# A hybrid decoder layer on one core: two row pairs of each output-projection half by Strassen's scheme

## The chip, the cores and the metric

The kernel runs on one core of a Trainium2 chip. The metric is the device time of one execution in microseconds (us); of several runs the median is given. TensorE (PE) multiplies, VectorE (DVE) and ScalarE (ACT) do the elementwise work, GpSimd (POOL) and SyncE (SP) here issue transfers. Each engine works through its own instructions in order.

## The reference

One layer on 256 rows of width 2048, all in float32. The change sits in the line `h = h + concat(A, B) @ w_o`, the output projection.

```python
a = rmsnorm(h, attn_norm[i])
proj = a @ w_in[i]                       # q, latent, rope key, q, k, v of two head groups
out_mla  = mla_attention(...)            # group A: 8 heads of 128
out_moba = moba_attention(...)           # group B: 8 heads of 128
h = h + jnp.concatenate([out_mla, out_moba], axis=-1) @ w_o[i]     # 2048 x 2048
f = rmsnorm(h, ffn_norm[i])
h = h + (jax.nn.silu(f @ w_gate[i]) * (f @ w_up[i])) @ w_down[i]   # inner width 5632
g = jax.nn.sigmoid(rmsnorm(h, ple_norm[i]) @ w_ple_gate[i])
h = h + g * (p[i] @ w_ple_proj[i])
return rmsnorm(h, final_norm)
```

## The kernel before

**Three matmuls for one.** Every float32 operand is split into a high part (rounded to the matmul's type fp32r) and a low part (what the rounding left). A product is three matmuls: high by high, low by high, high by low (lines 388, 389, 390). So each weight that comes from memory passes through ACT (the cast at line 337 writes the high part) and then DVE (the subtraction at line 348 writes the low part) before PE may use it.

**Units.** A matrix product is a `group`: 1024 columns of the weights, two row tiles of 128 tokens, and a list of units. A unit is a pair of 128-row blocks of the weights: 1 MB, loaded by SP into one of three buffers `raw` (tiles 112, 113 and 114 in the program; two more from the feed-forward part on). Its parts lie in a ring of 12 places of 512 columns (`ringh`, `ringl`); a group marked `deep` has four more places (`moreh`, `morel`). A plain unit takes four places and 24 matmuls of 512 columns.

**Strassen's scheme.** A unit is two blocks of weights by two halves of columns, against two by two blocks of activations, so Strassen's seven products can take the place of eight: 21 matmuls instead of 24. This asks for sums of the weights (lines 347, 350, 351, on DVE, in the buffer itself) which have to be split as well: seven places of the ring instead of four. It also asks for four sums of the activations (lines 140 to 143 in `act_transpose`, or `sums_of`), and at the end of a run of such units four additions that gather the products from PSUM into a tile `U` (lines 466 to 469). `seven` runs such a unit in four turns; its four extra PSUM banks are all that the other work has, so while a run lasts nothing else may take a bank. Before the change the feed-forward groups and the last projection use it; the output projection, `wo0` and `wo1` (columns 0 to 1023 and 1024 to 2047), consists of 16 plain units.

**Early sums.** For 13 of the feed-forward Strassen units the sums of the weights are made ahead: `early_sums` loads the weights by POOL's queue, adds on DVE (lines 372 to 374) and stores the sums to memory, from where they are loaded later. The last two of them (units 5 and 6 of `u4`, used near the end of the feed-forward part) are made while the output projection runs.

**Order around the change.** The output projection begins while the second attention group is still in its softmax. The values of the heads are multiplied between the first four units of `wo0` (lines 620, 621), and their parts `oB` are written by ACT and DVE (lines 106, 107). Tasks that wait for a turn (`add`, `step`) are woven between the units. When `wo0` is done, its four banks are added to the residual `h` (line 918), ACT sums the squares, and `ffn_norm_half(0)` takes the root of the norm, scales `h` (line 971), turns it on PE (line 123) and makes the parts and the sums of the next activations, one pair for each of the last units of `wo1`. When `wo1` is done the same happens for the second half, during the first units of the gate projection `g0`.

Of the kernel before, what the change touches and what calls it, by code (L numbers as in the profile page):

```python
# [8 lines left out]
F32 = mybir.dt.float32  # L9
# [4 lines left out]
ALU = mybir.AluOpType  # L14
# [21 lines left out]
def kernel(ctx, tc, x, w_in, w_ukv, w_o, w_gate, w_up, w_down, w_ple_gate, w_ple_proj,  # L36
                             final_norm, x_turned, p_turned, columns_in, out):
    nc = tc.nc
# [73 lines left out]
    def act_transpose(src, k0, g0, dst, kd0=None, scaled=False, sums=None):  # L112

        kd0 = k0 if kd0 is None else kd0
        part = src[:, :, k0 * 128:k0 * 128 + 256]
        if scaled:
            part = S["nrm"][:, (k0 // 2) % 2]
        b = obank()  # L120
        for i in range(2):
            for t in range(NT):
                nc.tensor.transpose(b[:, (2 * i + t) * 128:(2 * i + t + 1) * 128],  # L123
                                    part[:, t, i * 128:(i + 1) * 128], ident)
# [12 lines left out]
        a11, a21, a12, a22 = (whole[:, i, t * 128:(t + 1) * 128] for i in range(2) for t in range(2))
        four = some.rearrange("q a (b c) -> q (a b) c", b=2)
        tt = nc.vector.tensor_tensor
        tt(four[:, 0], a21, a22, op=ALU.add)  # L140
        tt(four[:, 2], a21, a11, op=ALU.subtract)
        tt(four[:, 1], four[:, 0], a11, op=ALU.subtract)
        tt(four[:, 3], a12, four[:, 1], op=ALU.subtract)
        split_psum(sums[0], sums[1], four)

    def square_sum(src, acc):
# [22 lines left out]
    units = []  # L169
# [169 lines left out]
    def split_lo(jb, c0=0, c1=None, n=1, row=slice(None)):  # L339

        if units[jb.unit].adding:
            return
        h, l, r = (x[:, row] for x in by_row_tile(n, *parts_of(jb), raw_of(jb)))
        tt = nc.vector.tensor_tensor
        f = quarters(jb) if jb.kind == "21" and not units[jb.unit].early else None
        if f is not None:
            tt(f[:, 0:2], f[:, 1:2].to_broadcast([128, 2, 512]), f[:, 0:4:3], op=ALU.subtract)  # L347
        tt(l[:, :, c0:c1], r[:, :, c0:c1], h[:, :, c0:c1].bitcast(F32), op=ALU.subtract)  # L348
        if f is not None:
            tt(f[:, 3], f[:, 3], f[:, 0], op=ALU.subtract)  # L350
            tt(f[:, 2], f[:, 2], f[:, 3], op=ALU.subtract)  # L351

    todo_early = []

    def early_sums(tag, enough, wait, landed=None):

        made = 0
        while todo_early and made < enough:
            u = todo_early.pop(0)
            made += 1  # L360
            f = big.tile([128, 4, 512], F32, name="wsums", tag=tag)
            (w, c0, _), k0 = u.srcs[0], u.ks[0] * 128
            if landed is not None:
                nc.gpsimd.tensor_copy(f[:, 0, 0:1], landed)
                landed = None
            nc.gpsimd.dma_start(f.rearrange("q (k a) c -> q k (a c)", k=2),
                                w[k0:k0 + 256, c0:c0 + 1024].rearrange("(k q) c -> q k c", q=128))
            since = columns[0]
            while columns[0] < since + wait() or S["crowded"]:
                yield 1  # L370
            tt = nc.vector.tensor_tensor
            tt(f[:, 0:2], f[:, 1:2].to_broadcast([128, 2, 512]), f[:, 0:4:3], op=ALU.subtract)
            tt(f[:, 3], f[:, 3], f[:, 0], op=ALU.subtract)
            tt(f[:, 2], f[:, 2], f[:, 3], op=ALU.subtract)
            u.early = dram.tile([128, 2048], F32, name=f"wsums{u.name}{u.idx}")
            nc.gpsimd.dma_start(u.early, f.rearrange("q a c -> q (a c)"))
# [65 lines left out]
    def seven(u, turn):  # L442
        st = u.st
        if turn == 0 and u.sevens_first:
            take_banks(u)
            n = B["next"] % 4
            st["free"] = B["rot"][n:] + B["rot"][:n]
            B["rot"], B["next"] = [st["banks"][1, 1]] if u.first else [], 0
            st.update(zip(("m1", "m7", "m5", "m6"), st["free"]))
        h, l = u.turns[turn][0].h, u.turns[turn][0].l  # L450
        k = u.ks[0]
        a11, a12, a22 = u.lhs(k, 0), u.lhs(k + 1, 0), u.lhs(k + 1, 1)
        s1, s2, s3, s4 = (u.sums(k, j) for j in range(4))
        todo = (((0, "m1", a11), (1, "m3", s4)), ((0, "m2", a12),), ((1, "m7", s3), (0, "m5", s1)),
                ((1, "m6", s2), (0, "m4", a22)))[turn]
        alone = {"m2": (0, 0), "m3": (1, 0), "m4": (0, 1)}
        for q, m, xs in todo:
            b = st["banks"][alone[m]] if m in alone else st[m]
            three(b, xs, h[:, 512 * q:512 * q + 512], l[:, 512 * q:512 * q + 512], begins(u, alone.get(m, m)),
                  u.sevens_end and m not in alone)  # L460
        if turn == 3 and u.sevens_end:
            U = S["U"] = big.tile([128, NT, 1024], F32, name="U", tag="vb")
            c1, c2 = U[:, :, 0:512], U[:, :, 512:1024]
            tt = nc.vector.tensor_tensor
            nc.scalar.copy(c1[:, 0], st["m1"])
            tt(c2[:, 0], c1[:, 0], st["m6"], op=ALU.add)
            tt(c1[:, 1], c2[:, 0], st["m7"], op=ALU.add)
            tt(c2[:, 0], c2[:, 0], st["m5"], op=ALU.add)
            tt(c2[:, 1], c1[:, 1], st["m5"], op=ALU.add)
            B["rot"], B["next"] = st["free"], 0  # L470
            if u.into is not None:
                def join(hs=S["h"][:, :, u.into:u.into + 1024]):
                    tt(hs, hs, U, op=ALU.add)
                    yield 1
                add(join())

    def sums_of(parts, k0, pairs, at, tag="vb"):

        for n, kk in enumerate(pairs):
            both = big.tile([128, 2, 2, SEQ], F32, name="both", tag=tag)  # L480
            whole, some = both[:, 0], both[:, 1]
            h, l = (x[:, kk - k0:kk - k0 + 2] for x in parts)
            tt = nc.vector.tensor_tensor
            tt(whole, h.bitcast(F32), l.bitcast(F32), op=ALU.add)
            a11, a21, a12, a22 = (whole[:, i, t * 128:(t + 1) * 128] for i in range(2) for t in range(2))
            hi, lo = (aT[i][:, at + 2 * n:at + 2 * n + 2] for i in range(2))
            four = some.rearrange("q a (b c) -> q (a b) c", b=2)
            tt(four[:, 0], a21, a22, op=ALU.add)
            tt(four[:, 1], four[:, 0], a11, op=ALU.subtract)
            tt(four[:, 2], a21, a11, op=ALU.subtract)  # L490
            tt(four[:, 3], a12, four[:, 1], op=ALU.subtract)
            split_psum(hi, lo, some)
            yield 1

# [9 lines left out]
    def add(gen, wait=0, front=False):  # L504
        tasks.insert(0 if front else len(tasks), [wait, gen])
# [450 lines left out]
    def ffn_norm_half(k0):  # L956

        def after():
            def g():
# [38 lines left out]
    def a_sums(k, j):  # L998
        return tuple(S["sums"][i][k // 2][:, j] for i in range(2))

    group("wo0", [(wo, 0, 1024)], K16, C2, o_l, add_evac(0, ssh, ffn_norm_half(0)))
    group("wo1", [(wo, 1024, 2048)], K16, C2, o_l, add_evac(1024, ssh, ffn_norm_half(8)), swap=True, deep=True)


    ffT = {}
# [323 lines left out]
    for i, u in enumerate(units):  # L1329
# [5 lines left out]
        S["long"] = u.name in ("ga", "q0", "u0", "wo0", "wo1")  # L1335
        S["crowded"] = u.name == "v" and u.idx > 0 or u.name == "wo0" and u.idx < 4
        if u.name == "ga" and u.idx == 5:
            todo_early.extend(x for x in units if x.early)
            add(early_sums("f0l", 2, lambda: 53248, raw[i + 3][:, 0, 0:1]))
        if u.name == "ga" and u.idx == 8:  # L1340
            add(early_sums("more_sums", 99, lambda: 57344 if S["long"] else 34816))
        if u.name == "g1" and u.idx == 0:
            S["mid"] = S.pop("turned")
        if u.name == "wo0":
# [87 lines left out]
```

## Time and profile before

| | |
|---|---|
| median of 3 runs | 1181.11 us (1179.98 to 1181.36) |
| the profiled execution | 1180.28 us, of which the span from first to last instruction is 1178.5 us |
| output projection on PE | first matmul at 285.27 us; `wo1` begins at 334.95 us |
| PE, DVE, ACT busy over the span | 99%, 81%, 60% |
| data moved | 287.80 MB, mean 244 GB/s |
| granted TensorE clock | 0.998 |

Times in the trace are microseconds from the start of the span. A row of the timeline gives start, duration, engine, line, operation, output and input tile, the shape, and how many equal instructions it merges; in brackets, how long the engine had stood idle and who ended that. A row of windows gives a stretch, its length, and the busy time of PE, PE's weight loads, DVE, ACT and POOL.

### The profile page before, as it was taken

The numbers are of one execution on the slowest core, as the hardware profiler recorded it, in microseconds if no ns is written. First come the engines' busy times: TensorE is split into PE (matmuls) and PEld (weight loads), VectorE is DVE, ScalarE is ACT, GpSimd is POOL, SyncE is SP. The second block draws the span as 40 slices with busy tenths as digits, with TensorE's granted clock in tenths as the row PEclk, the third lists the DMA queues.
The fourth block names the chain that finished last, engine by engine and source line by source line (L and its number), as shares of the span: only waits on it lengthen the run. The fifth ranks groups of instructions, "written<-read, shape, count | busy, mean of one in ns | idle before, by whom it ended". The sixth has DMA issues, their size and how long they took to land.

```text
span 1178.5 us, 14590 instructions
## 1 busy us (share of the span) xinstructions
PE 1167.4 (99%) x5477; PEld 978.3 (83%) x5477; DVE 952.9 (81%) x1127; ACT 710.7 (60%) x898; POOL 50.2 (4%) x73
## 2 busy tenths in 40 slices
PE   9999999999999999999999999999999999999996
PEld 7888888899888888888888888888888888888886
DVE  6866756776557689999999899989998989897474
ACT  6745746456456756667566666757575756465453
POOL 5000000000000000000000000000000000000000
PEclk9999999999999999999999999999999999999999
DMA  9896787755683776686959596868868795846531
GB/s 328 298 337 202 288 299 258 267 185 206 220 330 130 280 260 220 235 283 208 353 171 334 154 348 210 291 214 321 240 214 255 283 276 195 326 153 218 201 107 72
DMA packets 85880, 287.80 MB, mean 244 GB/s; under 512 B 5681, under 2 KB 7985, under 8 KB 81201
## 3 DMA queue, kind: packets, MB, share of 16 engines
q1 hardware_dynamic: 76352, 239.71, 56.7%
q0 software_dynamic: 8880, 46.14, 14.2%
q10 hardware_dynamic: 576, 1.02, 0.3%
q8 instruction: 43, 0.70, 0.2%
q14 instruction: 29, 0.23, 0.1%
HBM read 252.24 MB, written 26.21 MB: 236 GB/s over the span
## 4 chain that ended last, share of the span: by engine, by line
PE 95%; DMA 2%; ACT 1%; DVE 1%; SPq 0%; issue 0%; ACTq 0%; DVEq 0%
PE bank L390 30%; PE bank L388 30%; PE bank L389 30%; DMA raw<-in_w_in 2%; PE bank L591 1%; PE bank L1052 1%; PE bank L123 1%; PE bank L620 1%; ACT ringh L337 1%; PE bank L614 0%; PE bank L594 0%; PE bank L726 0%; DMA xT<-in_x_turned 0%; PE bank L621 0%; ACT aT L109 0%
## 5 line engine op out<-in xcount | busy, mean ns | idle before, releaser
L337 ACT CAST ringh<-raw 128x1024 fp32r<-128x1024 f32 (+5 forms) x310 | 372.7, 1239 | 274.9 <-PE bank L389 112.0
L348 DVE TENSOR_TENSOR ringl<-raw,ringh 128x1024 fp32r<-128x1024 f32 (+5 forms) x310 | 444.7, 1457 | 101.9 <-ACT ringh L337 100.0
L388 PE MATMUL bank<-ringh,aT 128*128 128x512 f32 (+3 forms) x713 | 274.7, 385 | 0.2
L390 PE MATMUL bank<-ringl,aT 128*128 128x512 f32 (+3 forms) x713 | 270.8, 380 | 0.0
L389 PE MATMUL bank<-ringh,aT 128*128 128x512 f32 (+3 forms) x713 | 270.3, 379 | 0.0
L390 PEld LDWEIGHTS bank<-ringl,aT 128*128 128x128 f32 x713 | 134.1, 188 | 25.3 <-DVE ringl L348 0.9
L388 PEld LDWEIGHTS bank<-ringh,aT 128*128 128x128 f32 x713 | 134.2, 188 | 24.7 <-ACT ringh L337 1.0
L389 PEld LDWEIGHTS bank<-ringh,aT 128*128 128x128 f32 x713 | 134.3, 188 | 23.8 <-DVE aT L658 0.2
L337 ACT CAST moreh<-raw 128x1024 fp32r<-128x1024 f32 (+2 forms) x70 | 79.8, 1173 | 19.9 <-DVE raw L347 9.2
L348 DVE TENSOR_TENSOR morel<-raw,moreh 128x1024 fp32r<-128x1024 f32 (+2 forms) x66 | 85.5, 1317 | 1.8 <-ACT moreh L337 1.3
L388 PE MATMUL bank<-ringh,ffTh 128*128 128x512 f32 x204 | 79.5, 390 | 0.0
L337 ACT CAST most<-raw 128x1024 fp32r<-128x1024 f32 (+2 forms) x58 | 56.8, 1005 | 37.5 <-DVE raw L347 14.4
L390 PE MATMUL bank<-ringl,ffTh 128*128 128x512 f32 x204 | 79.4, 389 | 0.0
L389 PE MATMUL bank<-ringh,ffTl 128*128 128x512 f32 x204 | 79.4, 389 | 0.0
L348 DVE TENSOR_TENSOR most<-raw,most 128x1024 fp32r<-128x1024 f32 (+2 forms) x58 | 66.3, 1164 | 1.6 <-ACT most L337 1.5
L347 DVE TENSOR_TENSOR raw<-raw 128x1024 f32<-128x1024 f32 x51 | 62.5, 1225 | 1.7
L389 PEld LDWEIGHTS bank<-ringh,ffTl 128*128 128x128 f32 x204 | 38.3, 188 | 8.0
L388 PEld LDWEIGHTS bank<-ringh,ffTh 128*128 128x128 f32 x204 | 38.3, 188 | 7.9
L390 PEld LDWEIGHTS bank<-ringl,ffTh 128*128 128x128 f32 x204 | 38.3, 188 | 7.9
L351 DVE TENSOR_TENSOR raw<-raw 128x512 f32<-128x512 f32 x51 | 35.3, 692 | 1.8
L350 DVE TENSOR_TENSOR raw<-raw 128x512 f32<-128x512 f32 x51 | 34.9, 684 | 0.0
L388 PE MATMUL bank<-most,aT 128*128 128x512 f32 x88 | 34.6, 394 | 0.0
(356 smaller groups left out, 1958.6 us busy)
## 6 DMA issues: line engine op xcount, KB each, us to landing
raw<-in_w_down SPq DMA_DIRECT2D x44, 1024.0 KB, 7.2
raw<-in_w_gate SPq DMA_DIRECT2D x35, 1024.0 KB, 7.4
raw<-in_w_up SPq DMA_DIRECT2D x32, 1024.0 KB, 7.5
raw<-in_w_in SPq DMA_DIRECT2D x40, 512.0 KB, 5.4
raw<-in_w_o SPq DMA_DIRECT2D x16, 1024.0 KB, 5.6
raw<-in_w_ple_gate SPq DMA_DIRECT2D x16, 1024.0 KB, 5.0
raw<-in_w_in SPq DMA_DIRECT2D x8, 1024.0 KB, 5.0
wsums<-in_w_up POOLq DMA_DIRECT2D x8, 1024.0 KB, 7.1
```

Of the source, the lines that this page charges most:

```text
L123: nc.tensor.transpose(b[:, (2 * i + t) * 128:(2 * i + t + 1) * 128], part[:, t, i * 128:(i + 1) * 128], ident)
L337: nc.scalar.copy(h[:, :, c0:c1], r[:, :, c0:c1])
L347: tt(f[:, 0:2], f[:, 1:2].to_broadcast([128, 2, 512]), f[:, 0:4:3], op=ALU.subtract)
L348: tt(l[:, :, c0:c1], r[:, :, c0:c1], h[:, :, c0:c1].bitcast(F32), op=ALU.subtract)
L350: tt(f[:, 3], f[:, 3], f[:, 0], op=ALU.subtract)
L351: tt(f[:, 2], f[:, 2], f[:, 3], op=ALU.subtract)
L388: nc.tensor.matmul(b, xh, h, start=start, stop=False)
L389: nc.tensor.matmul(b, xl, h, start=False, stop=False)
L390: nc.tensor.matmul(b, xh, l, start=False, stop=stop)
L591: nc.tensor.matmul(s[:, c0:c0 + nk], qT[:, q * 128:(q + 1) * 128], kT[:, 0:nk], start=True, stop=qpe is None)
L620: nc.tensor.matmul(o[:, 0:256], v(0), pT[:, 0:256], start=True, stop=False)
L1052: nc.tensor.transpose(b[:, (2 * i + t) * 128:(2 * i + t + 1) * 128], st[:, t, (k + i) * 128:(k + i + 1) * 128], ident)
```

## The change

Two units of `wo0` (heads 4 and 5, and 6 and 7, of the first attention group) and the same two of `wo1` become Strassen units, at places 4 and 5 of `wo0` and 2 and 3 of `wo1`. Their activations' sums are made by `sums_of` when `wo0` reaches its fourth and fifth unit, into a part of `aT` that is free then, and serve both halves. After each run the gathered tile `U` is added to `h` by one instruction (`join`). `ffn_norm_half(0)` takes its root and its first scaling as before, but leaves four turns before the first turning on PE, which so comes after the run. The signs of all of Strassen's sums are changed so that the weights' sums need only additions; with that the last two early units get their sums from six transfers each that copy and accumulate in memory (`early_by_transfers`, POOL's queue) instead of from DVE. Since the two groups now mix kinds, their plain units are split in halves of 1024 columns.

```diff
-        tt(four[:, 0], a21, a22, op=ALU.add)
-        tt(four[:, 2], a21, a11, op=ALU.subtract)
+        tt(four[:, 0], a21, a22, op=ALU.subtract)
+        tt(four[:, 2], a11, a21, op=ALU.subtract)
...
-            tt(f[:, 0:2], f[:, 1:2].to_broadcast([128, 2, 512]), f[:, 0:4:3], op=ALU.subtract)
+            tt(f[:, 0:2], f[:, 1:2].to_broadcast([128, 2, 512]), f[:, 0:4:3], op=ALU.add)
...
+    def early_by_transfers(them):
+        for u in them:
...
+            nc.gpsimd.dma_start(e[:, 0:4:3], b11.to_broadcast([128, 2, 512]))
+            nc.gpsimd.dma_start(e[:, 1:2], b22)
+            nc.gpsimd.dma_start(e[:, 2:3], b21)
+            nc.gpsimd.dma_start(e[:, 0:2], b12.to_broadcast([128, 2, 512]), accum_op=ALU.add)
+            nc.gpsimd.dma_start(e[:, 3:4], e[:, 1:2], accum_op=ALU.add)
+            nc.gpsimd.dma_start(e[:, 2:3], e[:, 3:4], accum_op=ALU.add)
...
-                add(join())
+                add(join(), 1 if u.name == "wo0" else 0)
...
-                yield 1
+                yield 1 if k0 else 4
...
-    group("wo0", [(wo, 0, 1024)], K16, C2, o_l, add_evac(0, ssh, ffn_norm_half(0)))
-    group("wo1", [(wo, 1024, 2048)], K16, C2, o_l, add_evac(1024, ssh, ffn_norm_half(8)), swap=True, deep=True)
+    O_SUMS = [4, 6]
+
+    def out_projection(col0, pairs, after, **kw):
+        pairs = pairs.split()
+        group(f"wo{col0 // 1024}", [(wo, col0, col0 + 1024)], [2 * int(x.strip("S+")) + i for x in pairs for i in range(2)],
+              C2, o_l, add_evac(col0, ssh, after), sums=sum_at(O_SUMS, 8),
+              sevens=tuple(i for i, x in enumerate(pairs) if x[0] == "S"), into=col0,
+              adding=tuple(i for i, x in enumerate(pairs) if x[-1] == "+"),
+              order=[(0, 0), (1, 0), (0, 1), (1, 1)], **kw)
+
+    out_projection(0, "0 1 4 5 S2 S3 6 7", ffn_norm_half(0))
+    out_projection(1024, "0 1 S2 S3 4 5 6 7", ffn_norm_half(8), deep=True)
...
+            todo_early.extend(late_early[:-2])
...
+        if u.name == "wo1" and u.idx == 2:
+            early_by_transfers(late_early[:1])
+        if u.name == "u0" and i > wide and u.idx == 0:
+            early_by_transfers(late_early[1:])
+        if u.name == "wo0" and u.idx in (3, 4):
+            n = u.idx - 3
+            add(sums_of(S["oM"], 0, O_SUMS[n:n + 1], 8 + 2 * n, "stage"))
```

On DVE, in `wo0` before, from the low parts of head 7 to the weights of the fifth to eighth unit (`ringl` from `raw`; `wsums` are the early sums):

```order
L107 TENSOR_TENSOR oBl<-bank_83,oBh 128x256
L348 TENSOR_TENSOR ringl<-raw_113,ringh 128x2048
L372 TENSOR_TENSOR wsums<-wsums 128x1024
L373 TENSOR_TENSOR wsums<-wsums 128x512
L374 TENSOR_TENSOR wsums<-wsums 128x512
L348 TENSOR_TENSOR ringl<-raw_114,ringh 128x2048
L348 TENSOR_TENSOR ringl<-raw_112,ringh 128x2048
```

The same place now, of which the second Strassen unit of `wo0` (buffer 113) makes up most, with the sums of its activations (`both`, lines 499 to 506) among its pieces:

```order
L348 TENSOR_TENSOR ringl<-raw_113,ringh 128x1024
L499 TENSOR_TENSOR both<-oMh,oMl 128x512
L503 TENSOR_TENSOR both<-both 128x128
L504 TENSOR_TENSOR both<-both 128x128
L505 TENSOR_TENSOR both<-both 128x128
L506 TENSOR_TENSOR both<-both 128x128
L107 TENSOR_TENSOR aT_86<-both,aT_85 128x512
L347 TENSOR_TENSOR raw_113<-raw_113 128x1024
L348 TENSOR_TENSOR ringl<-raw_113,ringh 128x512
L350 TENSOR_TENSOR raw_113<-raw_113 128x512
L351 TENSOR_TENSOR raw_113<-raw_113 128x512
L348 TENSOR_TENSOR ringl<-raw_113,ringh 128x1024 x2
```

One instruction of 2048 columns became twelve or more, and the three of the early sums are gone.

On ACT, in `wo1` before, around the first turning for the norm (`stage` from a bank is the turned pair):

```order
L971 ACTIVATE stage<-h,rs 128x256 x2
L337 CAST moreh<-raw_112 128x2048
L135 ACTIVATE stage<-bank_84,given 128x256 x2
L106 CAST aT_85<-stage 128x512
L106 CAST sumsatt<-stage 128x512
L971 ACTIVATE stage<-h,rs 128x256 x2
```

The same place now, behind the run of Strassen units (line 480 reads the first product into `U`; the buffers 112 and 113 hold the units at places 5 and 6):

```order
L986 ACTIVATE stage<-h,rs 128x256 x2
L337 CAST moreh<-raw_114 128x1024 x2
L480 COPY U<-bank_77 128x512
L337 CAST ringh<-raw_112 128x1024 x2
L337 CAST ringh<-raw_113 128x1024 x2
L135 ACTIVATE stage<-bank_77,given 128x256 x2
L106 CAST aT_85<-stage 128x512
L106 CAST sumsatt<-stage 128x512
L986 ACTIVATE stage<-h,rs 128x256 x2
```

The scaling moved ahead of the weights of three units, and the reading of the turned pair now stands behind the casts of a unit whose buffer (113) was the second Strassen unit's.

More of the change, by code (lines that the diff above doesn't have):

```diff
@@ L139, in act_transpose @@
         tt = nc.vector.tensor_tensor
-        tt(four[:, 0], a21, a22, op=ALU.add)
-        tt(four[:, 2], a21, a11, op=ALU.subtract)
+        tt(four[:, 0], a21, a22, op=ALU.subtract)
+        tt(four[:, 2], a11, a21, op=ALU.subtract)
         tt(four[:, 1], four[:, 0], a11, op=ALU.subtract)
-        tt(four[:, 3], a12, four[:, 1], op=ALU.subtract)
+        tt(four[:, 3], four[:, 1], a12, op=ALU.add)
         split_psum(sums[0], sums[1], four)
@@ L346, in split_lo @@
         if f is not None:
-            tt(f[:, 0:2], f[:, 1:2].to_broadcast([128, 2, 512]), f[:, 0:4:3], op=ALU.subtract)
+            tt(f[:, 0:2], f[:, 1:2].to_broadcast([128, 2, 512]), f[:, 0:4:3], op=ALU.add)
         tt(l[:, :, c0:c1], r[:, :, c0:c1], h[:, :, c0:c1].bitcast(F32), op=ALU.subtract)
         if f is not None:
-            tt(f[:, 3], f[:, 3], f[:, 0], op=ALU.subtract)
-            tt(f[:, 2], f[:, 2], f[:, 3], op=ALU.subtract)
+            tt(f[:, 3], f[:, 3], f[:, 0], op=ALU.add)
+            tt(f[:, 2], f[:, 2], f[:, 3], op=ALU.add)
     todo_early = []
@@ L371, in early_sums @@
             tt = nc.vector.tensor_tensor
-            tt(f[:, 0:2], f[:, 1:2].to_broadcast([128, 2, 512]), f[:, 0:4:3], op=ALU.subtract)
-            tt(f[:, 3], f[:, 3], f[:, 0], op=ALU.subtract)
-            tt(f[:, 2], f[:, 2], f[:, 3], op=ALU.subtract)
+            tt(f[:, 0:2], f[:, 1:2].to_broadcast([128, 2, 512]), f[:, 0:4:3], op=ALU.add)
+            tt(f[:, 3], f[:, 3], f[:, 0], op=ALU.add)
+            tt(f[:, 2], f[:, 2], f[:, 3], op=ALU.add)
             u.early = dram.tile([128, 2048], F32, name=f"wsums{u.name}{u.idx}")
             nc.gpsimd.dma_start(u.early, f.rearrange("q a c -> q (a c)"))
+    def early_by_transfers(them):
+        for u in them:
+            u.early = dram.tile([128, 2048], F32, name=f"wsums{u.name}{u.idx}")
+            e = u.early.rearrange("q (a c) -> q a c", a=4)
+            (w, c0, _), k0 = u.srcs[0], u.ks[0] * 128
+            b11, b12, b21, b22 = (w[k0 + 128 * k:k0 + 128 * k + 128, c0 + c:c0 + c + 512].rearrange(
+                "q (a c) -> q a c", a=1) for k in range(2) for c in (0, 512))
+            nc.gpsimd.dma_start(e[:, 0:4:3], b11.to_broadcast([128, 2, 512]))
[4 more added lines that the diff above has]
+            nc.gpsimd.dma_start(e[:, 2:3], e[:, 3:4], accum_op=ALU.add)
     def split(jb):
@@ L467, in seven @@
             tt(c1[:, 1], c2[:, 0], st["m7"], op=ALU.add)
-            tt(c2[:, 0], c2[:, 0], st["m5"], op=ALU.add)
-            tt(c2[:, 1], c1[:, 1], st["m5"], op=ALU.add)
+            tt(c2[:, 0], st["m5"], c2[:, 0], op=ALU.subtract)
+            tt(c2[:, 1], st["m5"], c1[:, 1], op=ALU.subtract)
             B["rot"], B["next"] = st["free"], 0
@@ L487, in sums_of @@
             four = some.rearrange("q a (b c) -> q (a b) c", b=2)
-            tt(four[:, 0], a21, a22, op=ALU.add)
+            tt(four[:, 0], a21, a22, op=ALU.subtract)
             tt(four[:, 1], four[:, 0], a11, op=ALU.subtract)
-            tt(four[:, 2], a21, a11, op=ALU.subtract)
-            tt(four[:, 3], a12, four[:, 1], op=ALU.subtract)
+            tt(four[:, 2], a11, a21, op=ALU.subtract)
+            tt(four[:, 3], four[:, 1], a12, op=ALU.add)
             split_psum(hi, lo, some)
@@ L1337 @@
         if u.name == "ga" and u.idx == 5:
-            todo_early.extend(x for x in units if x.early)
+            late_early = [x for x in units if x.early]
+            todo_early.extend(late_early[:-2])
+            late_early = late_early[-2:]
             add(early_sums("f0l", 2, lambda: 53248, raw[i + 3][:, 0, 0:1]))
```

## The prediction

> **What bounds the kernel now.** I read the page first: busy times, slices and the shares of the chain of waits.
>
> ```profile
> span 1178.5 us, 14590 instructions
> PE 1167.4 (99%) x5477; PEld 978.3 (83%) x5477; DVE 952.9 (81%) x1127; ACT 710.7 (60%) x898; POOL 50.2 (4%) x73
> PE   9999999999999999999999999999999999999996
> DVE  6866756776557689999999899989998989897474
> PE 95%; DMA 2%; ACT 1%; DVE 1%; SPq 0%; issue 0%; ACTq 0%; DVEq 0%
> ```
>
> PE bounds the kernel. DVE is second: in slices of 29.5 us it has gaps in the first 14 (to 412 us), which hold the output projection, and nearly none after that. So fewer matmuls save time only while DVE keeps up with a shorter PE. The waits of PE and the windows say how near that is:
>
> ```profile
> PE bank L99 <- DVE warm L1287: 2.0, 1, 2.0
> 302.70:382.15 79.45, 79.45 (x363) 65.78 (x362) 53.06 (x63) 42.19 (x55) 1.81 (x3) 1.00 0.66 237
> 471.00:594.00 123.00, 123.00 (x550) 101.91 (x549) 117.30 (x119) 80.73 (x90) 3.96 (x4) 1.00 0.78 265
> ```
>
> PE's one wait of any size is 2.0 us at the start. The first window is the stretch that the change alters: from the low parts of head 4 (DVE, 302.70) to the end of the four additions that close `wo1` (382.15). PE is busy for all of it, DVE for 53.06 us: 26.39 idle. The second window, inside `u0` and its neighbours, already has Strassen units: DVE works 117.30 of 123.00 us there, 95.4%, and PE still doesn't wait. Where the idle 26.39 us end matters, because the additions hand over to a chain that has no slack:
>
> ```profile
> 379.68 2.47 DVE L918 TENSOR_TENSOR h<-h,bank 128x512 f32<-128x512 f32 x4
> 380.39 0.63 ACT L148 ACTIVATE junk<-h 128x512 bf16<-128x512 f32 x1 [3.43 <-DVE h L918]
> 382.89 1.89 ACT L337 CAST ringh<-raw 128x2048 fp32r<-128x2048 f32 x1
> 384.69 1.70 ACT L971 ACTIVATE stage<-h,rs 128x256 f32<-128x256 f32 x4
> 385.72 0.40 PE L390 MATMUL bank<-morel,aT 128*128 128x512 f32 x1
> 385.95 0.60 PE L123 MATMUL bank<-ident,stage 128*128 128x128 f32 x4
> ```
>
> Additions, squares, scaling, turning: PE's turning at 385.95 follows the matmul at 385.72 at once, and the scaling that it reads began at 384.69. DVE later than 382.15 is PE later, almost one for one.
>
> **The change part by part.** *PE.* Each Strassen unit has 21 matmuls for 24, so 12 go.
>
> ```profile
> 313.19 0.39 PE L388 MATMUL bank<-ringh,oBh 128*128 128x512 f32 x1
> 327.47 0.39 PE L388 MATMUL bank<-ringh,oBh 128*128 128x512 f32 x1
> ```
>
> There are 64 matmuls from the first to the second: (327.47 − 313.19)/63 = 0.2267 us each. 12 × 0.2267 = **−2.72 us**. On time, DVE's stretch would now end at 382.15 − 2.72 = 379.43: 76.7 us are there.
>
> *DVE, weights.* A plain unit is one subtraction of 2048 columns; a Strassen unit of a feed-forward group shows what replaces it:
>
> ```profile
> 377.47 2.29 DVE L348 TENSOR_TENSOR ringl<-raw,ringh 128x2048 fp32r<-128x2048 f32 x1
> 420.89 1.22 DVE L348 TENSOR_TENSOR ringl<-raw,ringh 128x1024 fp32r<-128x1024 f32 x1 [0.60 <-ACT ringh L337]
> 424.61 0.69 DVE L351 TENSOR_TENSOR raw<-raw 128x512 f32<-128x512 f32 x1
> 427.81 2.36 DVE L348 TENSOR_TENSOR ringl<-raw,ringh 128x1024 fp32r<-128x1024 f32 x2 [2.51 <-ACT ringh L337]
> ```
>
> From 420.89 to 424.61 + 0.69 are 4.41 us, and 2.36 for the last two pieces: 6.8 for 2.29, **+4.5** per unit, four units **+18.0**. Eight plain units in halves cost 2.36 − 2.29 = 0.07 each, **+0.6**.
>
> *DVE, activations.* A turned pair has the same addition of four blocks and the same low part as `sums_of`:
>
> ```profile
> 353.43 0.69 DVE L107 TENSOR_TENSOR aT<-stage,aT 128x512 fp32r<-128x512 f32 x1 [4.16 <-ACT aT L106]
> 355.75 0.69 DVE L107 TENSOR_TENSOR sumsatt<-stage,sumsatt 128x512 fp32r<-128x512 f32 x1 [0.69 <-ACT sumsatt L106]
> 356.35 2.28 DVE L348 TENSOR_TENSOR morel<-raw,moreh 128x2048 fp32r<-128x2048 f32 x1
> 359.74 0.69 DVE L107 TENSOR_TENSOR aT<-stage,aT 128x512 fp32r<-128x512 f32 x1 [1.10 <-ACT aT L106]
> 362.05 0.69 DVE L107 TENSOR_TENSOR sumsatt<-stage,sumsatt 128x512 fp32r<-128x512 f32 x1 [0.69 <-ACT sumsatt L106]
> ```
>
> One takes 353.43 to 356.35 = 2.9 us, its wait for ACT's cast (0.69) included, since DVE stands behind it: two, **+5.8**.
>
> *DVE, gathering; early sums.*
>
> ```profile
> 507.14 0.68 DVE L466 TENSOR_TENSOR U<-U,bank 128x512 f32<-128x512 f32 x1
> 509.78 2.28 DVE L348 TENSOR_TENSOR morel<-raw,moreh 128x2048 fp32r<-128x2048 f32 x1
> 311.96 1.22 DVE L372 TENSOR_TENSOR wsums<-wsums 128x1024 f32<-128x1024 f32 x1
> 313.94 0.69 DVE L374 TENSOR_TENSOR wsums<-wsums 128x512 f32<-128x512 f32 x1
> ```
>
> Gathering is 509.78 − 507.14 = 2.64 per run, **+5.3**; a join adds 2048 columns, the stride 377.47 to 379.68 = 2.2, two **+4.4**. The early sums that leave this stretch, 311.96 to 313.94 + 0.69 = 2.67 per unit, two: **−5.3**. Sum on DVE: 18.0 + 0.6 + 5.8 + 5.3 + 4.4 − 5.3 = **+28.8**.
>
> *Waits of DVE that stay.* 53.06 + 28.8 = 81.9 us of work already exceed 76.7. The idle time doesn't all vanish either. DVE's order is fixed, and each of the four turned pairs of `wo1` puts two casts of ACT in its way, at 359.74 (1.10) and 362.05 (0.69), with nothing between that could run: 4 × 1.79 = **7.2**. DVE needs 53.06 + 28.8 + 7.2 = 89.1 us and ends at 302.70 + 89.1 = 391.8, against 382.15: **+9.6 us**. The 2.72 of PE are already gone in it, since the end is DVE's.
>
> *New waits, estimated.* Three new ones, for which these rows give the price:
>
> ```profile
> 340.28 1.28 ACT L157 ACT_TABLE_LOAD   x1
> 412.19 1.99 ACT L337 CAST moreh<-raw 128x1024 fp32r<-128x1024 f32 x2
> raw<-in_w_o SPq DMA_DIRECT2D x16, 1024.0 KB, 5.6
> raw<-in_w_gate SPq DMA_DIRECT2D x35, 1024.0 KB, 7.4
> ```
>
> The cast of the first Strassen unit of `wo1` now stands on ACT behind the four squares: 382.89 − 380.39 = 2.50, then one cast (1.0), while DVE has three additions left (1.8): 1.7. The norm's root with its table load (1.28) is ahead of the run on ACT, where DVE waits for pieces of a Strassen unit: 0.8 of it. And buffer 113 comes free only with the last piece of the second Strassen unit of `wo1`; its next load takes 5.6, and the two casts of it are ahead of the reading of the turned pair and of the next scaling on ACT: 0.7 for DVE. Together **+3.2**; from below 0 (if DVE's lateness covers them), from above 1.8 more at each of the two runs, if loads land in 7.4 as those of the gate projection.
>
> *Transfers on POOL.* Six per unit replace DVE's sums.
>
> ```profile
> 239.14 0.55 POOL L376 DMA_DIRECT2D wsumsu<-wsums  x1 [10.16 <-DVE wsums L374]
> 510.44 0.90 POOL L1018 DMA_DIRECT2D stage<-U  x1 [166.22 <-DVE U L469]
> wsumsu<-wsums POOLq DMA_DIRECT2D x8, 1024.0 KB, 4.8
> morel<-raw POOLq DMA_DIRECT2D x4, 1024.0 KB, 11.5
> ```
>
> They wait for no other engine, so POOL gives them out from its store at 239.14 on. POOL's next own work is at 510.44. Each lands in 4.8 to 11.5 us, so six in a row take 29 to 69, both units 58 to 138: done by 378 at the latest, and the sums are read near the end of the feed-forward part. I price them at nothing; what they could cost, slower loads of `w_o` beside them, is in the bound above. The loads of `h` (now behind one another), the roots and the scaling are the same instructions in other places, and cost nothing of their own.
>
> Sum: +9.6 + 3.2 = **+12.8 us**. The profiled execution took 1180.28, so 1193.1; the median of the runs is 0.83 above it: **1193.9, about 1194**. I expect PE to wait some 15.5 us (12.8 + 2.72): at the second Strassen unit of each half, ahead of the turnings in the last units of `wo1`, and at the first turnings of `g0`.
>
> **The rivals.** *DVE is late, but its waits fill.* A late DVE finds ACT's casts of the turned pairs done, but for the round trip of 0.69 in each pair: 53.06 + 28.8 + 4 × 0.69 = 84.7; it ends at 387.4, +5.2, and without the three new waits 1186.3. For it: ACT has 42.19 of 79.45 us to do. Against it: the first wait of each pair follows PE's turning, which itself follows DVE's last step.
>
> *Faster: PE keeps the lead.* DVE works in the changed stretch as densely as from 471 to 594, 95.4%, and PE's 2.72 us are kept: 1180.28 − 2.72 + 0.83 = 1178.4. It decides if DVE needs at most 0.954 × 76.7 = 73.2 us; the rows give 81.9 before any wait, 8.7 too much. It would need the Strassen units to cost DVE about half of 4.5 each, or the slack behind 385.95 to open.
>
> *Slower still: the waits themselves cost clock, or loads land late.*
>
> ```profile
> 5.28 0.77 PE L388 MATMUL bank<-ringh,aT 128*128 128x512 f32 x1
> 7.33 0.46 PE L389 MATMUL bank<-ringh,aT 128*128 128x512 f32 x1
> ```
>
> After its 2.0 us of waiting PE's first four matmuls took 7.33 − 5.28 = 2.05 us, against 4 × 0.2267 = 0.91: 1.14 lost. If that comes again behind each of three or four long waits, it is 3.4 to 4.6 more: 1197.3 to 1198.5. Loads in 7.4 us at the two runs give 1193.9 + 3.6 = 1197.5. The windows show a granted clock of 1.00, and no row of before shows PE idle for long behind its start.
>
> [...]
>
> **How the numbers follow.** A measurement can tell about 0.2% (2.4 us) from no change. DVE as the bound with its waits, 1190 to 1197: 57%, since its terms are counted instructions with durations of like rows. The waits fill, 1184 to 1189: 22%. Clock or loads, 1197 to 1200: 10%. Faster at 1178.4: 6%, one of them inside 0.2%. Something between that and the filled waits, within 0.2%: 5%. So faster 0.05, same 0.06, slower 0.89. The range 1184.5 to 1199 leaves out the faster and the unchanged case, and the ends of two others, together under 2 in 10.
>
> **What would show it.** In the profile after: 12 matmuls fewer; DVE's busy time from head 4's low parts to the additions of `wo1` about 82 us, and almost no idle time but behind ACT's casts; waits of PE of 13 to 18 us, for DVE's low parts and ACT's scaling, all between 300 and 410 us; from 470 us on everything the same, only later. It would be wrong if DVE's busy time is below 77 there, if PE's waits are under 5 us, if the additions of `wo1` end before 385, or if time is lost in `u4`, where the transferred sums are read.

## The result, and the profile after

The changed kernel took 1194.77 us (median of four runs, 1192.27 to 1195.42), the kernel before 1180.82 beside it: a ratio of 1.0115, 95% interval 1.0097 to 1.0132. It is slower by about 14 us; forecast were 1194.0, 13.2 more than 1180.82.

The page of the changed kernel: span, busy times, the slices of DVE and of the granted clock.

```profile
span 1193.3 us, 14681 instructions
PE 1172.7 (98%) x5465; PEld 979.1 (82%) x5465; DVE 980.0 (82%) x1179; ACT 720.4 (60%) x926; POOL 57.2 (5%) x81
DVE  7866756875888679999989899989998999897474
PEclk9999999999998999999999999999999999999999
```

PE has its 12 matmuls fewer (5477 to 5465), and yet it is busy for 5.3 us more (1167.4 before) and idle for 9.5 us more (1193.3 − 1172.7 = 20.6 for 1178.5 − 1167.4 = 11.1). So matmuls took longer as well, and one slice of the clock's row has dropped. (Rows of matmuls overlap, 0.39 long at a stride of 0.2267, so stalls up to about 0.16 us also count as busy.) The waits of PE in the changed kernel (engine and line, who was waited for: sum, times, longest):

```profile
PE bank L123 <- ACT stage L986: 4.9, 2, 2.5
PE bank L405 <- DVE ringl L348: 3.5, 4, 1.2
PE bank L99 <- DVE warm L1312: 2.0, 1, 2.0
```

The one of 2.0 was there before. The new ones are for DVE's low parts in the second Strassen unit of each run and for ACT's scaling ahead of a turning. All lost time lies ahead of one matmul of the gate projection: the same matmul just behind the altered stretch, and one near the end, before and after.

```profile
429.81 0.39 PE L390 MATMUL bank<-morel,aT 128*128 128x512 f32 x1
1157.73 0.39 PE L390 MATMUL bank<-wfl,aT 128*128 128x512 f32 x1
```

```profile
444.70 0.39 PE L405 MATMUL bank<-morel,aT 128*128 128x512 f32 x1
1172.62 0.39 PE L405 MATMUL bank<-wfl,aT 128*128 128x512 f32 x1
```

Both are 14.89 us later. With the 2.72 us of the missing matmuls 17.6 us have to be found. The next rows are the second turning of `wo1` and what follows it:

```profile
368.12 0.39 PE L405 MATMUL bank<-morel,oBh 128*128 128x512 f32 x1
371.02 0.95 PE L123 MATMUL bank<-ident,stage 128*128 128x128 f32 x4 [2.52 <-ACT stage L986]
373.10 0.63 PE L404 MATMUL bank<-ringh,oBl 128*128 128x512 f32 x1
376.84 0.39 PE L403 MATMUL bank<-ringh,oBh 128*128 128x512 f32 x1
```

PE waits 2.5 us, then a matmul takes 0.63 instead of 0.39: the rows stand 0.43 apart instead of 0.2267 until 375.7. The windows name the cause in their column of the clock (the number behind the busy times of PE, its loads, DVE, ACT and POOL):

```profile
358.64:362.05 3.41, 3.41 (x9) 2.63 (x9) 2.89 (x3) 3.41 (x6) 0.00 (x0) 0.50 0.35 67
372.29:375.70 3.41, 3.41 (x10) 2.64 (x9) 3.41 (x4) 2.31 (x5) 0.00 (x0) 0.50 0.00 0
399.60:403.01 3.41, 3.41 (x11) 2.73 (x10) 1.22 (x1) 3.41 (x4) 0.00 (x0) 0.50 1.04 414
```

Three times the clock falls to half, for 3.41 us each: behind the second Strassen unit of `wo1` (waits of 1.1, 0.35, 0.3 and 1.4 us within 5.6), behind this turning, and behind the first turning of `g0` (2.5). Each costs 7 or 8 matmuls × 0.2 = about 1.6 us, 4.7 together. The account of the 17.6: 0.8 ahead of the stretch, 1.9 at the second unit of `wo0`, 3.1 at that of `wo1`, 2.7 at the second turning, 2.9 at the first of `g0`, 4.7 by the clock; about 1.5 is spread over smaller stalls, the slower turnings behind the waits among them.

DVE in the same stretch as in the prediction (from the low parts of head 4 to the end of the additions of `wo1`), whole and cut where the additions of `wo0` end; before first, then after:

```profile
302.70:335.84 33.14, 33.14 (x151) 27.60 (x150) 20.26 (x17) 12.44 (x14) 1.26 (x2) 1.00 0.84 310
335.84:382.15 46.31, 46.31 (x213) 38.18 (x212) 32.81 (x46) 29.75 (x41) 0.55 (x1) 1.00 0.53 186
```

```profile
303.51:395.87 92.36, 86.06 (x366) 68.33 (x365) 79.63 (x111) 51.84 (x78) 0.00 (x0) 0.96 0.52 180
303.51:341.58 38.07, 36.75 (x163) 29.72 (x162) 35.46 (x47) 17.77 (x25) 0.00 (x0) 1.00 0.62 219
341.58:395.87 54.29, 49.31 (x205) 38.60 (x204) 44.17 (x64) 34.07 (x54) 0.00 (x0) 0.94 0.45 154
```

79.63 us of work (81.9 were forecast) and 12.7 of waiting (10.4), the end at 395.87 (391.8, and 395.0 with the new waits). Each half has become longer: the first by 4.9, the second by 8.0 us. Two of the waits that the forecast had priced as new stand in these rows, at the first Strassen unit of `wo1` (1.7 forecast) and at the norm's root (0.8):

```profile
343.38 1.22 DVE L348 TENSOR_TENSOR morel<-raw,moreh 128x1024 fp32r<-128x1024 f32 x1 [1.81 <-ACT moreh L337]
351.95 0.17 DVE L159 RECIPROCAL rs_y<-rs_s 128x2 f32<-128x2 f32 x1 [1.48 <-ACT rs_s L157]
```

PE's first turning of `g0`, to which DVE hands over at the end of this stretch, came at 385.95 before and now comes 13.0 us later:

```profile
398.96 1.12 PE L123 MATMUL bank<-ident,stage 128*128 128x128 f32 x4 [2.37 <-ACT stage L986]
```

The other 1.9 of the 14.89 us are lost behind it, most of them by the third fall of the clock.

### The profile page after: what moved, and what is told of

It reads as the page before. It is cut to its first block, busy times and chain, and to the rows that moved or that the text cites. A ratio compares the mean times of both kernels' runs of the same rounds, so it can differ in the third digit from the quotient of the medians.

```text
span 1193.3 us, 14681 instructions
## 1 busy us (share of the span) xinstructions
PE 1172.7 (98%) x5465; PEld 979.1 (82%) x5465; DVE 980.0 (82%) x1179; ACT 720.4 (60%) x926; POOL 57.2 (5%) x81
## 3 DMA queue, kind: packets, MB, share of 16 engines
q0 software_dynamic: 9776, 46.14, 14.8%
## 4 chain that ended last, share of the span: by engine, by line
PE 87%; DVE 5%; ACT 4%; DMA 2%; issue 1%; POOL 0%; ACTq 0%; DVEq 0%; POOLq 0%
PE bank L403 28%; PE bank L405 28%; PE bank L404 28%; DVE ringl L348 2%; DMA raw<-in_w_o 2%; ACT ringh L337 2%; PE bank L1077 1%; PE bank L123 1%; DMA raw<-in_w_in 1%; PE bank L606 0%; PE bank L609 0%; DVE raw L347 0%; ACT junk L148 0%; ACT att L619 0%; PE bank L741 0%
## 5 line engine op out<-in xcount | busy, mean ns | idle before, releaser
L337 ACT CAST ringh<-raw 128x1024 fp32r<-128x1024 f32 (+4 forms) x332 | 381.1, 1186 | 285.3 <-PE bank L404 100.8
L348 DVE TENSOR_TENSOR ringl<-raw,ringh 128x1024 fp32r<-128x1024 f32 (+4 forms) x332 | 453.8, 1391 | 93.8 <-ACT ringh L337 91.8
L403 PE MATMUL bank<-ringh,aT 128*128 128x512 f32 (+3 forms) x728 | 281.8, 387 | 0.6 <-ACT stage L875 0.4
L405 PE MATMUL bank<-ringl,aT 128*128 128x512 f32 (+3 forms) x728 | 277.9, 382 | 2.4 <-DVE ringl L348 2.4
L404 PE MATMUL bank<-ringh,aT 128*128 128x512 f32 (+3 forms) x728 | 277.1, 381 | 0.0
L405 PEld LDWEIGHTS bank<-ringl,aT 128*128 128x128 f32 x728 | 137.5, 189 | 29.2 <-DVE ringl L348 4.0
L403 PEld LDWEIGHTS bank<-ringh,aT 128*128 128x128 f32 x728 | 137.7, 189 | 26.2 <-ACT ringh L337 1.7
L404 PEld LDWEIGHTS bank<-ringh,aT 128*128 128x128 f32 x728 | 137.7, 189 | 24.4 <-DVE aT L673 0.2
L347 DVE TENSOR_TENSOR raw<-raw 128x1024 f32<-128x1024 f32 x55 | 67.4, 1225 | 1.8
L351 DVE TENSOR_TENSOR raw<-raw 128x512 f32<-128x512 f32 x55 | 38.1, 692 | 1.9
L350 DVE TENSOR_TENSOR raw<-raw 128x512 f32<-128x512 f32 x55 | 37.6, 684 | 0.0
```

The source lines that it names most:

```text
L337: nc.scalar.copy(h[:, :, c0:c1], r[:, :, c0:c1])
L350: tt(f[:, 3], f[:, 3], f[:, 0], op=ALU.add)
L351: tt(f[:, 2], f[:, 2], f[:, 3], op=ALU.add)
L403: nc.tensor.matmul(b, xh, h, start=start, stop=False)
L404: nc.tensor.matmul(b, xl, h, start=False, stop=False)
L405: nc.tensor.matmul(b, xh, l, start=False, stop=stop)
```

## The experiments

Theory A: VectorE's time sets the end. Rival B: the transfers disturb the work beside them. Rival C: the loss is made by the turnings' place among ScalarE's casts. Times are medians; ratios are to the kernel before on the same chip.

**transfers.** `wo0` and `wo1` plain as before; early sums and signs as after.

```diff
-                yield 1 if k0 else 4
+                yield 1
...
-    out_projection(0, "0 1 4 5 S2 S3 6 7", ffn_norm_half(0))
-    out_projection(1024, "0 1 S2 S3 4 5 6 7", ffn_norm_half(8), deep=True)
+    group("wo0", [(wo, 0, 1024)], K16, C2, o_l, add_evac(0, ssh, ffn_norm_half(0)))
+    group("wo1", [(wo, 1024, 2048)], K16, C2, o_l, add_evac(1024, ssh, ffn_norm_half(8)), swap=True, deep=True)
...
-        if u.name == "wo0" and u.idx in (3, 4):
-            n = u.idx - 3
-            add(sums_of(S["oM"], 0, O_SUMS[n:n + 1], 8 + 2 * n, "stage"))
```

> The two early units' sums by transfers and the turned signs alone; the output projection is plain as before. Theory A (VectorE's time in the output projection is what the change lacks): PE never waited in this stretch before, and VectorE only loses 5.3 us of work, so no change, 1180.8 within 1 us. Theory B (the twelve transfers slow the loads or the attention beside them; the first low part of head 4 came 0.8 us later after the change): 0.8 to 3 us slower, 1181.6 to 1184, with the loss between 239 and 303 us.

1181.66 us, ratio 1.0010 (1.0001 to 1.0019): about 1.1 us slower, just clear of no change. The same matmul behind the values of the heads, before and in this kernel:

```profile
300.19 0.47 PE L388 MATMUL bank<-ringh,oMh 128*128 128x512 f32 x1
```

```profile
301.55 0.47 PE L403 MATMUL bank<-ringh,oMh 128*128 128x512 f32 x1
```

It comes 1.36 us later, and the delay does not grow after that. B holds for about 1 us of the 14. Whether the transfers themselves do it or the other order on DVE during the softmax stays open: this kernel has both. POOL gives the transfers out when the forecast said; the last one in the changed kernel:

```profile
292.28 0.81 POOL L391 DMA_DIRECT2D wsumsu<-wsumsu  x1 [6.21 <-DMA wsumsu<-wsumsu]
```

**half0.** Strassen units in `wo0` alone.

```diff
-                yield 1 if k0 else 4
+                yield 1
...
-    out_projection(1024, "0 1 S2 S3 4 5 6 7", ffn_norm_half(8), deep=True)
+    group("wo1", [(wo, 1024, 2048)], K16, C2, o_l, add_evac(1024, ssh, ffn_norm_half(8)), swap=True, deep=True)
```

> Strassen units in the first half (wo0) alone; wo1 plain, its turnings as before. Theory A: VectorE's work in the stretch is 53.06 + 2 x 4.5 + 5.8 + 2.6 + 2.2 + 0.3 - 5.3 = 67.7, with 7.2 of waits 74.9 of 78.1 us, so it is on time at the end, but the second unit of the run still waits as in the changed kernel (about 2 to 2.5 us at 320 to 324): 1180.8 - 1.36 + 2 to 4 = 1181.5 to 1183.5, clock 1.00. Theory C (the loss is made at the turnings of the second half, where ScalarE's scalings stand behind casts of late buffers): the same or 1179.5. Theory B: 1182 to 1184 with the loss ahead of 303 us.

1183.49 us, ratio 1.0027 (1.0017 to 1.0036). Its windows, cut as above:

```profile
304.20:342.04 37.84, 36.52 (x162) 29.53 (x161) 35.33 (x45) 17.60 (x23) 0.00 (x0) 1.00 0.62 222
342.04:384.32 42.28, 42.28 (x196) 34.84 (x195) 28.17 (x42) 28.27 (x42) 0.00 (x0) 1.00 0.48 168
```

DVE fills the first half (35.33 of 37.84) and is late by 4.7 there; the plain second half gives part of it back, in 42.28 instead of 46.31 us. By the distances of its rows PE waits 1.9 us in the second unit of the run and 0.6 at the first turning of `g0`. The clock stays at 1.00, as A forecast. But the matmul behind the values of the heads, at 300.19 before, is already late in the profiled execution of this kernel:

```profile
302.05 0.48 PE L403 MATMUL bank<-ringh,oBh 128*128 128x512 f32 x1
```

That is 1.86 us, more than with the transfers alone. So the time fits A and B alike, and the rows show some of both.

**half1.** Strassen units in `wo1` alone.

```diff
-    out_projection(0, "0 1 4 5 S2 S3 6 7", ffn_norm_half(0))
+    group("wo0", [(wo, 0, 1024)], K16, C2, o_l, add_evac(0, ssh, ffn_norm_half(0)))
```

> Strassen units in the second half (wo1) alone; wo0 plain. Theory A by the whole stretch: 74.9 of 78.1 us, on time, 1179.5 to 1182. Theory C: the waits at the second unit, at the second turning and at the first turning of g0 all stay, 8 to 11 us, and the low clock behind them (3 to 5 us): 1180.8 - 1.36 + 11 to 16 = 1190 to 1195. In between, 1184 to 1188, if the lateness that wo0 hands over makes up half of it.

1195.43 us, ratio 1.0128 (1.0112 to 1.0144): as much lost as by the whole change, with half of it. This is what speaks against one budget for the whole stretch: by it, DVE would be on time. Its second half:

```profile
337.07:388.74 51.67, 46.68 (x199) 37.50 (x197) 39.77 (x62) 30.61 (x50) 0.00 (x0) 0.93 0.39 128
```

And the waits of PE in it:

```profile
PE bank L403 <- ACT moreh L337: 4.2, 1, 4.2
PE bank L123 <- ACT stage L986: 3.1, 1, 3.1
```

The additions end at 388.74, 6.6 later than before, though `wo0` left DVE its idle time. But it isn't a clean cut: ACT now casts the first weights of `g0` behind the squares, which wait for those additions. That is the wait of 4.2, and it is not in the changed kernel. So the experiment speaks against the single budget, without proving it wrong by itself, and doesn't tell A from C.

**nosums.** The weights of the four Strassen units are not added up.

```diff
         f = quarters(jb) if jb.kind == "21" and not units[jb.unit].early else None
+        if units[jb.unit].name[:2] == "wo":
+            f = None
```

> The changed kernel without VectorE's additions of the weights in the four Strassen units (the products there then use blocks that were never summed: that part of the computation is left out). Takes 4 x 2.6 = 10.4 us off VectorE and leaves PE, ScalarE and all orders alone. Theory A: the end of the stretch comes about 10 us earlier, PE's waits fall to 3 to 7 us, and most of the low clock goes: 1182 to 1186. Theory C (orders on ScalarE): little changes, 1190 or more. Theory B: 1192 or more.

1187.35 us, ratio 1.0056 (1.0042 to 1.0071): about 7 us less than the changed kernel for 10.4 us less work on DVE (an estimate, four units by 2.6). The additions of `wo1`:

```profile
386.57 2.47 DVE L935 TENSOR_TENSOR h<-h,bank 128x512 f32<-128x512 f32 x4
```

The waits of PE for scalings:

```profile
PE bank L123 <- ACT stage L988: 4.8, 3, 2.4
```

The additions end 6.8 us earlier, and PE's waits for low parts are gone. The waits for scalings stay, three of together 4.8 us. More came back than C allows, and less than A said. DVE still has some 16 us more to do than before (26.6 − 10.4); how much of the 6.8 us that are left is that work and how much the order isn't told apart by this kernel.

**twoscales.** Both scalings ahead of the first turning.

```diff
                 scale(k0)
-                if k0:
-                    scale(k0 + 2)
+                scale(k0 + 2)
...
-                    nx = k + (4 if k0 else 2)
+                    nx = k + 4
```

> The changed kernel with the scalings of both of the first two pairs ahead of the first turning, so that the second turning (2.5 us of waiting and 1.7 us of low clock in the changed kernel) no longer waits behind ScalarE's casts. Theory A (VectorE's work in the second half sets the end): that wait goes and turns up later, at the first unit or the first turning of g0, since VectorE still has the same to do: 1193 to 1195.5, the additions of wo1 end as late as before this edit. Theory C (the turnings' place on ScalarE makes the loss): 4.4 us less, about 1190.4.

1194.5 us, ratio 1.0115 (1.0100 to 1.0130): no change. The additions of `wo1` begin 0.6 us earlier than in the changed kernel, where they begin at 393.40:

```profile
392.83 2.48 DVE L933 TENSOR_TENSOR h<-h,bank 128x512 f32<-128x512 f32 x4
```

The wait of 2.5 us at the second turning is gone. One of 1.4 has come at the first turning, and the one at the first turning of `g0` has grown from 2.4 to 5.7:

```profile
PE bank L123 <- ACT stage L986: 5.7, 1, 5.7
```

That is as A forecast: a wait that is taken away where DVE isn't relieved turns up at the next places. C falls as the main cause.

**filler.** Idle matmuls where PE waits.

```diff
+    FILL = {2: 11, 8: 11}
...
         b = obank()
+        for _ in range(FILL.get(k0, 0) if scaled else 0):
+            nc.tensor.matmul(b, S["oM"][0][:, 0, 0:128], S["oM"][0][:, 0:2, :].rearrange("q a b -> q (a b)"), start=True, stop=True)
```

> The changed kernel with eleven idle matmuls (results overwritten) on PE ahead of the second turning and eleven ahead of the first turning of g0, where PE otherwise waits 2.5 us each. They fill 11 x 0.2267 = 2.5 us, so nothing else moves but the clock. If the low clock behind these two waits is a loss of its own: it goes there (granted clock 1.00 at 372 to 376 and 399 to 403 us), 1.7 + 1.8 us, of which the second is kept in full and the first only if VectorE is not what PE meets next: 1191 to 1193. If the low clock is hidden by VectorE's lateness everywhere: 1194.5, no change. If the clock's falls have another cause, the low rows stay: 1194.5.

1193.15 us, ratio 1.0106 (1.0091 to 1.0121). The interval overlaps that of the changed kernel, so the time alone doesn't prove the gain of 1.6; the windows around the two places show the step:

```profile
372.00:376.00 4.00, 4.00 (x19) 3.29 (x18) 4.00 (x4) 2.36 (x5) 0.00 (x0) 1.00 0.00 0
399.50:404.00 4.50, 4.50 (x22) 3.73 (x21) 1.08 (x1) 4.50 (x5) 0.00 (x0) 1.00 1.03 411
```

The clock stays at 1.00 in both places, so it is the waiting that makes it fall there. It also stays at 1.00 behind the second Strassen unit of `wo1`, where nothing was filled and PE's waits come to 2.9 us within 5.4, so not all that this kernel's profile gains is the filling's work. All three falls, 4.7 us, are gone, and the time is 1.6 us less. And the additions of `wo1`:

```profile
393.14 2.48 DVE L936 TENSOR_TENSOR h<-h,bank 128x512 f32<-128x512 f32 x4
```

They begin 0.3 us earlier than in the changed kernel: a faster PE hardly helps while DVE is behind.

**load96, load48b.** The kernel before with idle additions on VectorE. Their tile stood among the others:

```diff
+    spare = big.tile([128, 224], F32, name="spare")
+    nc.vector.memset(spare, 0.0)
+    LOAD = {(g, i): 12 for g, r in (("wo0", range(4, 8)), ("wo1", range(0, 4))) for i in r}
...
+        for _ in range(LOAD.get((u.name, u.idx), 0)):
+            nc.vector.tensor_tensor(spare, spare, spare, op=ALU.add)
```

> The kernel before, with 96 idle additions of 224 columns on VectorE (about 0.31 us each, 29.8 us in all, near the 28.8 of the change), twelve at each of the last four units of wo0 and the first four of wo1; nothing else is touched, PE keeps its 12 matmuls. Theory A, one budget for the whole stretch: 53.06 + 29.8 + 7.2 = 90.1 for 79.45, +10.6: 1191. Theory A', a budget for each half (wo0: 20.26 busy of 33.14; wo1: 32.81 of 46.31): 20.3 + 14.9 + 2 for 33.1 and 32.8 + 14.9 + 7.5 for 46.3, +4 and +9: 1193.5, and up to 5 more from low clock. A rival by which the Strassen units' own steps (sums, banks, places) make the loss and not VectorE's time: 1181 to 1184.

> The kernel before, with 48 such additions (14.9 us), twelve at each of the first four units of wo1, none in wo0. One budget for the whole stretch: 53.06 + 14.9 + 7.2 = 75.2 for 79.45, so no change: 1180.5 to 1181.5. A budget for each half: 32.8 + 14.9 + 7.5 = 55.2 for 46.3, +8.9: 1189.5, with low clock up to 1194.

1217.68 us, ratio 1.0313 (1.0295 to 1.0330), and 1208.43, ratio 1.0235 (1.0220 to 1.0250): far more than any theory said. Two things were off. One addition takes 0.42 us to the next, not 0.31. And PE was slower to the end of the program, a stride of 0.232 instead of 0.227. The next kernels allow for both.

**load64, load36.** The same with fewer additions (8 at each of the eight units; 9 at each of the first four of `wo1`), and with the tile behind all others.

```diff
-    spare = big.tile([128, 224], F32, name="spare")
+    spare = small.tile([128, 224], F32, name="spare", tag="spare", bufs=1)
```

> As load96, with 64 idle additions (0.42 us from one to the next in load96, so 26.9 us, near the 28.8 of the change), eight at each of the last four units of wo0 and the first four of wo1, and with the additions' tile put behind all others, so that no other tile lies elsewhere than before. One budget: 53.06 + 26.9 + 7.2 = 87.2 for 79.45: +7.7. A budget for each half: wo0 20.3 + 13.4 + 2 for 33.1, wo1 32.8 + 13.4 + 7.5 for 46.3: +2.6 and +7.4, together +10, with low clock 1190.5 to 1196. If the Strassen units' own steps make the loss and not VectorE's time: 1181.

> 36 such additions (15.1 us), nine at each of the first four units of wo1, none in wo0. One budget for the whole stretch: 53.06 + 15.1 + 7.2 = 75.4 for 79.45: no change, 1181. A budget for each half: 32.8 + 15.1 + 7.5 = 55.4 for 46.3: +9.1, with low clock 1190 to 1195.

load64: 1190.7 us, ratio 1.0090 (1.0072 to 1.0108), +10.3. load36: 1189.36 us, ratio 1.0073 (1.0057 to 1.0089), +8.9. By one budget load36 would cost nothing; by the half's own budget +9.1. The additions of `wo1` in load64, 9.8 us later than before:

```profile
389.45 2.47 DVE L921 TENSOR_TENSOR h<-h,bank 128x512 f32<-128x512 f32 x4
```

In load36 the second half, to the end of those additions:

```profile
336.48:391.37 54.89, 48.23 (x213) 39.48 (x212) 46.38 (x82) 29.79 (x41) 0.55 (x1) 0.94 0.45 157
```

And PE's wait there, for the scaling ahead of a turning:

```profile
PE bank L126 <- ACT stage L974: 6.7, 1, 6.7
```

46.38 us of work in 54.89, where before it was 32.81 in 46.31: idle time in the first half was of no use to the second, and DVE's time alone, with no Strassen unit in the output projection, makes PE wait for a scaling and the clock fall (0.94). The stretch that counts may be shorter still than a half. All 36 additions stand ahead of the sums of the first turned pair, for which ACT waits 8.6 us before it comes to the next scaling:

```profile
363.58 0.62 ACT L109 CAST sumsatt<-stage 128x512 fp32r<-128x512 f32 x1 [8.59 <-DVE stage L146]
```

Additions at the last units of `wo1` were not tried.

**placed, placed512.** The kernel before with a tile that nothing uses, of 896 and of 512 bytes of each partition, ahead of the buffers.

```diff
+    spare = big.tile([128, 224], F32, name="spare")
+    nc.vector.memset(spare, 0.0)
```

> The kernel before with the additions' tile of load96 (896 bytes of each partition) where it stood there, ahead of the buffers and the ring, written once and not used: most later tiles lie 896 bytes further on, and nothing else changes. In load96 and load48b matmuls followed one another by 0.232 us instead of 0.227, to the end of the program, long behind the last added work. If the place of the tiles makes that: 1180.7 x (1 + 0.025 x about 0.8) = 1195 to 1204, though the program does nothing more. If VectorE's added work made it: 1181.

> As placed, with a tile of 512 bytes of each partition instead of 896. If any move of the tiles slows the matmuls: again 1190 to 1200. If the slowdown hangs on how far they are moved: another time, 1180 if 512 bytes are a step that the order of the memory repeats, and a shorter one if the kernel before happens not to lie at its best.

With 896 bytes 1195.23 us, ratio 1.0124 (1.0108 to 1.0140); with 512 bytes 1180.59, ratio 1.0000 (0.9990 to 1.0009). The window of 123 us from the prediction, in the kernel with 896 and in that with 512 bytes:

```profile
471.00:594.00 123.00, 123.00 (x542) 100.42 (x541) 117.77 (x120) 79.61 (x87) 2.87 (x3) 1.00 0.79 262
```

```profile
471.00:594.00 123.00, 123.00 (x550) 101.86 (x549) 118.01 (x120) 81.15 (x90) 3.60 (x4) 1.00 0.79 265
```

PE gets through 542 instructions for 550, without a gap and the clock at 1.00 in both. So the place of the tiles alone costs 14.8 us. load96 and load48b have the same tile in the same place and the same longer stride (less the 14.8, load48b would be at 1193.6, nearer to what was expected).

## Why the prediction was right, and where it was not

- **PE, −2.72 us.** The 12 matmuls are gone, but the saving never shows, as forecast: where DVE sets the end, a shorter PE only waits longer (idle for 20.6 us, where it was 11.1 before).
- **DVE, +28.8 us of work.** Measured +26.6 (79.63 − 53.06). Of the 2.2 too much, 1.4 are the two waits of 0.69 that the term for the activations counted in.
- **Waits of DVE, 7.2 + 3.2.** Measured 12.7 in all: 5.7 at ACT's casts of the turned pairs (7.2 forecast), 1.81 and 1.48 at the first two new places (1.7 and 0.8), twice 0.69 at the sums of the activations, the rest in small ones. Work and waits together are 92.4 us, and 92.3 were forecast. That they agree so closely is luck in part: less work and more waiting cancel.
- **The order beside the work.** With about as much idle work and no Strassen unit in the output projection (load64) the loss is 10.3; in the changed kernel about 14. No run divides the difference of 4 between the waits in the new order, the clock and the transfers.
- **One budget of 76.7 us: the step that failed.** The prediction set 89.1 us against 76.7 for `wo0` and `wo1` together. load36 and half1 are within such a budget and lose 8.9 and 14.9 us. Idle time in `wo0` was of no use for `wo1`. The likely reason, which no run tests, is that DVE takes its instructions in order and those of `wo1` follow PE's progress: before, DVE stood idle for 4.16 us until 353.43, though the cast that its next weights (356.35) read had ended at 348.30, and what it stood for was a pair that ACT could read only after 3.61 us of waiting for PE's turning. Set up by halves, the measured need was 38.07 us where 33.14 had done and 54.29 where 46.31 had done. The sum came out because in this change both halves are short; with work added to one half alone, as in load36, it would not have.
- **PE's waits of 15.5 us: wrong in size.** The waits shown come to 9.4 us beside the old one of 2.0 (4.9 + 3.5 and two of 0.6 and 0.4), below the 13 to 18 that were named. 4.7 us were lost to the clock instead, which stood in the prediction as a rival on top of the sum, with 10% for it and for late loads, and with the forecast on its own at 57%. What came is a mixture. PE's first turning of `g0` is 13.0 us later, as the forecast of 12.8 by DVE's lateness has it; the third fall of the clock comes on top. The first two seem to be hidden in that lateness: filler is rid of all three and gains 1.6 us. The places named for the waits were right for all the large ones.
- **Transfers at nothing.** About 1.1 us too little; the loss lies ahead of the stretch that was added up, which begins 0.8 us later (303.51 for 302.70).
- **The faster rival** needed 73.2 us of DVE's time; it had 79.63 of work alone. **Waits fill** (1186): DVE's waits didn't shrink (12.7 us where the rival had 2.8); the first cast of each pair follows PE's turning, which follows DVE, as the prediction held against it.

On the clock, the rows first. In the changed kernel it is halved from 358.64, 372.29 and 399.60 on, for 3.41 us each; the starts are 13.65 and 27.31 us apart, 4 and 8 times 3.41. In the 3.41 us ahead of each fall PE was busy for 1.98, 1.20 and 0.97 us. The waits of 1.9 us within 3.3 at the second unit of `wo0` left it at 1.00, but in twoscales the same waits at the same place halved it:

```profile
324.84:328.25 3.41, 3.41 (x9) 2.65 (x9) 3.41 (x4) 3.41 (x5) 0.00 (x0) 0.50 0.76 252
```

PE had work in the stretch ahead of each fall, and each fall ended after 3.41 us in which PE was busy throughout (3.41 of 3.41); how much less work lets the clock fall is not settled by these runs, and neither is what sets the steps of 3.41 us. The changed kernel's runs spread from 1192.27 to 1195.42, with a mean clock of 0.997 in the fastest and 0.993 to 0.995 in the others. So the same waits cost clock in one execution (0.50 in twoscales) and not in another (1.00 in the changed kernel). The 1.14 us at the start of the kernel before, from which the rival on the clock took its price, are no such fall: over 5.28 to 7.33 us the granted clock was 1.00.

No version here beats the kernel before. The best that keeps Strassen units in the output projection is half0, 2.9 us slower.

## What to carry to other kernels

Before work is moved to the second busiest engine, count its idle time stretch by stretch, between the points where it hands over to the bound engine, and not over a longer window: 13.5 us of idle time in `wo1` were not enough for 15.1 us of additions, though 26.4 us were idle in both halves together (load36, 8.9 us slower). Where that engine had become the bound, taking away one wait only moved it to the next places (twoscales: one of 2.5 us went, one of 1.4 came and one grew from 2.4 to 5.7, the time staying at 1194.5), so relieve the engine or leave it. A short wait of TensorE cost twice here, once as waiting and once as low clock behind it (2.4 us of waiting and then 3.41 us at half clock), but not all of the second was in the time: without the three falls, 4.7 us, filler took 1.6 us less.

## What was not expected of the hardware

An unused tile of 896 bytes of each partition ahead of the others made the unchanged program 14.8 us slower (1195.23, ratio 1.0124), by a longer stride of matmuls at a granted clock of 1.00 (from 479.83 to 491.87 us 52 strides of 0.2315, where 0.2267 was measured before); one of 512 bytes changed nothing. Which operand's place it is was not tried. An experiment that adds a tile should put it behind all others, or be compared with the tile alone.
